# A two-layer encoder on one core: split weight tiles in rows of 136 elements instead of 128

## The chip, the cores and the metric

The kernel runs on one core of one Trainium2 chip, as one launch. TensorE (PE) multiplies, VectorE (DVE) and ScalarE (ACT) prepare operands and take results away, GpSimd (POOL) builds a few tables, and SyncE (SP) issues the loads. The on-chip memory SBUF has 128 partitions; an address in it is given here as bytes from the start of a partition. PSUM takes the products.

The metric is the device time of the launch in microseconds. Before the change the median of two runs is 2129.01 us (2128.55 to 2129.46).

## The reference

An encoder of two layers over 256 tokens and 2048 features, in float32:

```python
def reference(x, attn_norm, mlp_norm, w_mlp_in, w_mlp_out, even_w_in, even_rpb, even_w_out,
              odd_w_qkv, odd_sink, odd_w_out, final_norm):
    for i in range(DEPTH):
        h = rms_norm(x, attn_norm[i])
        j = i // 2
        if i % 2 == 0:
            x = x + even_mixer(h, even_w_in[j], even_rpb[j], even_w_out[j])
        else:
            x = x + odd_mixer(h, odd_w_qkv[j], odd_sink[j], odd_w_out[j])
        x = x + sq_relu_mlp(rms_norm(x, mlp_norm[i]), w_mlp_in[i], w_mlp_out[i])
    return rms_norm(x, final_norm)
```

A mixer is a projection to queries, keys and values, attention with 16 heads of 128 (neighbourhood and dilated windows in layer 0, a window of 128 tokens with grouped keys in layer 1), and a projection back. The MLP is `relu(h @ w1)` squared, times `w2`, with 8192 hidden features. Nearly all the arithmetic is in the weight products.

## The kernel before, in words

Features lie on partitions, tokens along the row. A product's weights are the stationary operand, a tile of 128 x 128 (a k-tile is one such tile of the contraction); the activations of 256 tokens stream past it. To keep float32 accuracy from products of the type float32r, each operand is split into an upper part (rounded to float32r) and a lower one (the rest). Upper and lower parts of an activation lie side by side, so one product with the weights' upper part `h` streams 512 columns (L142), and a second with the weights' lower part `l` streams the upper activations alone, 256 columns (L144). The names of the streamed tiles tell the stage: `u` (normed input of a projection or of the MLP's first product), `hid` (the MLP's hidden features), `o` (heads' outputs). A weight unit, 16 k-tiles and one column block of output, goes through `unit` or `some_units` and `k_range`.

Weights come in halves of a unit: `take_half` issues one load of 512 KB into a tile `r` (SP, six buffers) and splits it into `h` (ACT, L81) and `l` (DVE, L82), five buffers each, up to three halves ahead of their use. A few units at stage changes keep their last two k-tiles in tiles of their own, `hh` and `hl`. At the start three units run in step with the first loads (L463 and L465).

Value projections work the other way round (`value_pair`, L264): the activations are stationary, and two k-tile places of `h` or `l` side by side stream as 256 columns, which needs the half as one flat run of 1024 elements.

Everything is emitted by plain loops, and each engine works through its own queue in that order. Attention's steps are put some steps later into the same order (`later`, `tick`).

Where the tiles lie, as the built program places them: `u` starts at byte 32,896, k-tile k of it 2048k further; `h` tiles at 99,744 plus multiples of 4096, `l` tiles at 120,224 plus multiples of 4096, k-tile k in them 512k further; `hid` and `o` start at 158,208, again 2048 per k-tile. Modulo 512 that is 128 for `u`, 0 for `hid` and `o`, and 416 for every k-tile of weights.

Of the kernel before, what the change touches and what calls it, by code (L numbers as in the profile page):

```python
# [8 lines left out]
F32R = mybir.dt.float32r  # L9
# [5 lines left out]
P = 128  # L15
T = 256
# [8 lines left out]
SCALE = 128.0 ** -0.5  # L25
TW = 384
HALF = KT // 2
RAW_BUFS = 6
PART_BUFS = 5
# steps between the stages of a head's attention  # L30
LAGS_0 = (5,4,3)
LAGS_1 = (4,5,3)
LAGS_END = (3,3,2)
# [7 lines left out]
def encoder(ctx: ExitStack, tc: tile.TileContext, a: dict, outT: bass.AP):  # L41
# [4 lines left out]
    whi = ctx.enter_context(tc.tile_pool(name="whi", bufs=PART_BUFS))  # L46
    wlo = ctx.enter_context(tc.tile_pool(name="wlo", bufs=PART_BUFS))
    held_w = ctx.enter_context(tc.tile_pool(name="held_w", bufs=3))
    work = ctx.enter_context(tc.tile_pool(name="work", bufs=3))
    acc_ps = ctx.enter_context(tc.tile_pool(name="acc_ps", bufs=3, space=PSUM))  # L50
    aux_ps = ctx.enter_context(tc.tile_pool(name="aux_ps", bufs=1, space=PSUM))

# [1 line left out]
    xs = const.tile([P, KT, T], F32, name="xs")  # L54
    u = const.tile([P, KT, 2, T], F32R, name="u")
    g = const.tile([P, 5, KT], F32, name="g")
# [15 lines left out]
    nc.vector.memset(eps, EPS)  # L72

    def warm(func, after):
        # has the function's table loaded ahead of its use
        nc.scalar.activation(warmed, after, func)

    warm(AF.Sqrt, eps)
# [1 line left out]
    def split(hi, lo, src):  # L80
        nc.scalar.activation(hi, src, AF.Copy)  # L81
        nc.vector.tensor_sub(lo, src, hi.bitcast(F32))  # L82

# [1 line left out]
    AHEAD = 2  # L85
    pending = []
    loaded = []

    def need(units, held=0):
        # of the first `held` units the last two k-tiles get tiles of their own  # L90
        for i, src in enumerate(units):
            pending.extend([(src[:, :HALF, :], HALF), (src[:, HALF:, :], HALF - 2 if i < held else HALF)])

    def take_half():
        while pending and len(loaded) <= AHEAD:
            src, n = pending.pop(0)
            r = raw.tile([P, HALF, P], F32, name="r")
            nc.sync.dma_start(r, src)
            h = whi.tile([P, HALF, P], F32R, name="h")
            l = wlo.tile([P, HALF, P], F32R, name="l")  # L100
            split(h[:, :n, :], l[:, :n, :], r[:, :n, :])
            tiles = [(h[:, k, :], l[:, k, :]) for k in range(n)]
            if n < HALF:
                h, l = (held_w.tile([P, 2, P], F32R, name=name) for name in ("hh", "hl"))
                split(h, l, r[:, n:, :])
                tiles += [(h[:, k, :], l[:, k, :]) for k in range(2)]
            loaded.append((h, l, tiles))
        return loaded.pop(0)
# [1 line left out]
    def take_unit():  # L110
        return take_half()[2] + take_half()[2]

# [1 line left out]
    now = [0]  # L114
    tasks = []

# [35 lines left out]
        done(ps)  # L152

    def some_units(done, act):
        # the last k-tiles of the activations become ready late: leave them for the end
        ps = [acc_ps.tile([P, 2 * T], F32, name="acc") for _ in done]
        parts = []
        for i in range(len(done)):
            parts.append(take_unit())
            if act is not u:  # L160
                assert heads_done >= set(range(KT - 2))
            k_range(ps[i], parts[i], act, range(KT - 2))
        if act is not u:
            finish_tasks()
        for i in range(len(done)):
            k_range(ps[i], parts[i], act, range(KT - 2, KT))
            done[i](ps[i])
# [5 lines left out]
        nc.vector.tensor_add(z, ps[:, :T], t)  # L173
        return z

# [1 line left out]
    def gained(k, which):  # L177
        x, gk = xs[:, k, :], g[:, which, k:k + 1]
        if which == 4:
# [14 lines left out]
    norm = {"ready": False, "waiting": []}  # L194

    def finish_norm(last=None, to=None):
        # mean square with tokens on partitions, 1/rms there, and the same along every partition
        ps = aux_ps.tile([P, 512], F32, name="m_ps", bufs=2)
        parts = [ssq] if last is None else [ssq, last]
        for j in range(2):  # L200
            for n, part in enumerate(parts):
                nc.tensor.matmul(ps[:, j:j + 1], part[:, j * P:(j + 1) * P], ones[:, 0:1],
                                 start=n == 0, stop=n == len(parts) - 1)
        r0, v, e = (work.tile([P, 2], F32, name=n, bufs=1) for n in ("r0", "v", "e"))
        nc.scalar.activation(r0, ps[:, :2], AF.Sqrt, bias=eps, scale=1.0 / D)
        nc.vector.tensor_scalar(v, ps[:, :2], 1.0 / D, EPS, op0=ALU.mult, op1=ALU.add)
        nc.vector.reciprocal(r0, r0)
        nc.vector.scalar_tensor_tensor(e, r0, -0.5, r0, op0=ALU.mult, op1=ALU.mult)
        nc.vector.tensor_mul(e, e, v)
        nc.vector.scalar_tensor_tensor(rcol, e, 1.5, r0, op0=ALU.add, op1=ALU.mult)  # L210
        diag = work.tile([P, 2, P], F32, name="diag", bufs=1)
        for j in range(2):
            nc.vector.tensor_scalar(diag[:, j, :], ident, rcol[:, j:j + 1], None, op0=ALU.mult)

        def along():
            out = aux_ps.tile([P, 512], F32, name="m_ps", bufs=2)
            nc.tensor.matmul(out[:, :T], ones, diag.rearrange("p j t -> p (j t)"), start=True, stop=True)
            to(out[:, :T])
        return along
# [13 lines left out]
        later(2, finish_norm(to=to))  # L233
        norm["ready"] = False

# [1 line left out]
    def head_parts(pool, name, bufs, scale, keep):  # L237
        def done(ps):
            z = joined(ps)
# [11 lines left out]
        return done  # L251

    def value_pair(pool, keep):
        # tokens on partitions, two heads at a time
        ps = acc_ps.tile([P, 2, T], F32, name="acc")
        for half in range(2):
            parts = [take_half()[:2] for _ in range(2)]
            for kk in range(HALF):
                k = half * HALF + kk
                h, l = (w.rearrange("p k c -> p (k c)")[:, (kk % 4) * T:(kk % 4 + 1) * T] for w in parts[kk // 4])  # L260
                for j in range(2):
                    js = slice(j * P, (j + 1) * P)
                    for n, (x, y) in enumerate(((0, h), (0, l), (1, h))):
                        nc.tensor.matmul(ps[:, j, :], u[:, k, x, js], y,  # L264
                                         start=k == 0 and j == 0 and n == 0,
                                         stop=k == KT - 1 and n == 2, skip_group_check=True)
                if kk % 2 == 1:
                    tick()
        assert norm["ready"]
        w = pool.tile([P, 2, 2, T], F32R, name="v", bufs=1)  # L270
        for j in range(2):
            nc.scalar.activation(w[:, 0, j, :], ps[:, j, :], AF.Copy, scale=rcol[:, j:j + 1])
            nc.vector.scalar_tensor_tensor(w[:, 1, j, :], ps[:, j, :], rcol[:, j:j + 1],
                                           w[:, 0, j, :].bitcast(F32), op0=ALU.mult, op1=ALU.subtract)
        keep.append(w)

    def attend(pool, o, head, q, k, v, side, biases, lags, sunk=False):
        """q, k, v: lists that hold the operands once their units are done."""
        def scores():
            if not q or not k:  # L280
                later(1, scores)
# [120 lines left out]
                    final = which_next == 4 and b == 1 and c == KT - 1  # L402
                    unit(added(c, final), hid, srcs=2, summed=final)

# [1 line left out]
    w0, w1 = a["even_w_in"], a["odd_w_qkv"]  # L406
    for p in range(8):
        base = 2 * p if p < 4 else 24 + 2 * (p - 4)
        for i in range(2):
            need([w0[base + i], w0[base + 8 + i]])  # L410
        need([a["even_w_v"][p, i] for i in range(2)])
    need([a["even_w_out"][c] for c in range(KT)], 3)

    def mlp_units(layer):
# [5 lines left out]
    mlp_units(0)  # L420
    for p in range(2):
        need([w1[NH + 2 * p + i] for i in range(2)], 2 if p == 0 else 0)
        need([a["odd_w_v"][p, i] for i in range(2)])
        need([w1[8 * p + i] for i in range(8)])
    need([a["odd_w_out"][c] for c in range(KT)], 3)
    mlp_units(1)

# [1 line left out]
    wps = aux_ps.tile([P, 512], F32, name="m_ps", bufs=2)  # L429
    for _ in range(10):  # L430
        nc.tensor.matmul(wps[:, :P], ones, ones, start=True, stop=True)

# [1 line left out]
    STARTERS = 3  # L434
    GROUPS = ((0, 2), (2, 4), (4, 8), (8, 12), (12, 16))
    starters = [[pending.pop(0)[0] for _ in range(2)] for _ in range(STARTERS)]
# [12 lines left out]
    hl = [None] * STARTERS  # L449
    for k0, k1 in GROUPS:  # L450
        ks = slice(k0 % HALF, (k1 - 1) % HALF + 1)
        if k0 % HALF == 0:
            hl = [(whi.tile([P, HALF, P], F32R, name="h"), wlo.tile([P, HALF, P], F32R, name="l"))
                  for _ in range(STARTERS)]
        for i in range(STARTERS):
            split(hl[i][0][:, ks, :], hl[i][1][:, ks, :], rs[k0 // HALF][i][:, ks, :])
# [3 lines left out]
        for i in range(STARTERS):  # L460
            h, l = hl[i]
            for k in range(k0, k1):
                nc.tensor.matmul(sps[i], h[:, k % HALF, :], u[:, k].rearrange("p a t -> p (a t)"),  # L463
                                 start=k == 0, stop=False)
# [9 lines left out]
        later(1 + gi, some_squares(gi))  # L474
    later(8, norm_for_heads)

# [1 line left out]
    with tc.tile_pool(name="attn0", bufs=1) as pool:  # L478
        o = pool.tile([P, NH, 2, T], F32R, name="o")
        sl = slopes(8)  # L480
# [22 lines left out]
        for p in range(8):  # L503
            q, k, v = [[], []], [[], []], []
# [15 lines left out]
        finish_tasks()  # L520
    mlp(0, 2)

# [1 line left out]
    with tc.tile_pool(name="attn1", bufs=1) as pool:  # L524
        o = pool.tile([P, NH, 2, T], F32R, name="o")
        sl = slopes(16)
# [28 lines left out]

    mlp(1, 4)

# [1 line left out]
    def to(r):  # L559
        for k0, k1 in ((0, 1), (1, 2)) + tuple((k, k + 2) for k in range(2, KT, 2)):  # L560
            ks = slice(k0, k1)
# [70 lines left out]
```

## Time and profile before

| | |
|---|---|
| median of the runs | 2129.01 us |
| profiled execution, span from first to last instruction | 2127.8 us |
| PE busy | 2104.8 us (99%), 12438 products |
| DVE busy | 1340.4 us (63%) |
| ACT busy | 1035.6 us (49%) |
| DMA | 386.06 MB, mean 181 GB/s |
| mean granted TensorE clock | 0.994 |

The profiled execution is a run of its own; the profile gives its span, and no other time of it is known. PE is the matrix engine's products, PEld its weight loads, which overlap products. Products are pipelined and the ends that the profile shows for them are modelled, so a product's pace is read from the starts of neighbours. The granted clock is 1.00 at the level of 2.4 GHz and 0.50 at that of 1.2 GHz.

### The profile page before, as it was taken

How to read it: one execution, taken by the hardware profiler on the slowest of the kernel's cores; microseconds unless marked ns; L12 is line 12 of the kernel's file. 1: busy time of each engine (PE TensorE's matmuls, PEld its weight loads, DVE VectorE, ACT ScalarE, POOL GpSimd, SP SyncE). 2: the span in 40 equal slices, each digit the busy share in tenths (PEclk: the TensorE clock that was granted, in tenths of full speed). 3: DMA queues.
4: the chain of work that ended last, by engine and by line, in shares of the span. 5: the costliest groups of instructions: out<-in, count | busy, mean ns of one | idle time of the engine just before them, and what ended most of it. 6: DMA issues, size and time to landing. Idle time of an engine off the chain costs nothing.

```text
span 2127.8 us, 31825 instructions
## 1 busy us (share of the span) xinstructions
PE 2104.8 (99%) x12438; PEld 1852.0 (87%) x12438; DVE 1340.4 (63%) x2088; ACT 1035.6 (49%) x1602; POOL 23.2 (1%) x33
## 2 busy tenths in 40 slices
PE   8999999999999999999999999999999999999997
PEld 6999998888888888888888998888888888888887
DVE  6766676766655556665656877766655556665554
ACT  6555555544444444444445656544444444444442
POOL 2100000000000000000000000000000000000000
PEclk9999999999999999999999999999999999999998
DMA  9754455555555555555555444555555555555552
GB/s 258 180 171 168 168 170 176 190 180 188 187 187 188 188 186 185 187 187 189 188 188 187 148 162 143 188 185 188 185 187 187 188 188 186 187 188 188 188 188 90
DMA packets 108294, 386.06 MB, mean 181 GB/s; under 512 B 12352, under 2 KB 13392, under 8 KB 108144
## 3 DMA queue, kind: packets, MB, share of 16 engines
q1 hardware_dynamic: 106992, 381.73, 53.2%
q0 software_dynamic: 1008, 2.27, 1.5%
q8 instruction: 97, 1.59, 0.3%
q14 instruction: 53, 0.43, 0.1%
q10 hardware_dynamic: 144, 0.04, 0.0%
HBM read 381.89 MB, written 2.10 MB: 180 GB/s over the span
## 4 chain that ended last, share of the span: by engine, by line
PE 96%; DMA 2%; DVE 1%; SPq 0%; ACT 0%; issue 0%; DVEq 0%; ACTq 0%
PE acc L142 58%; PE acc L144 30%; PE acc L264 5%; PE s_ps L288 1%; PE m_ps L332 1%; DMA r<-in_even_w_in 1%; PE p_ps L313 1%; DMA r<-in_even_w_v 1%; DMA xs<-in_xT 0%; ACT h L81 0%; DVE l L82 0%; DVE xs L562 0%; SPq L440 0%; PE acc L140 0%; PE acc L139 0%
## 5 line engine op out<-in xcount | busy, mean ns | idle before, releaser
L82 DVE TENSOR_TENSOR l<-r,h 128x1024 fp32r<-128x1024 f32 (+3 forms) x729 | 880.8, 1209 | 718.4 <-ACT h L81 716.3
L81 ACT ACTIVATE h<-r 128x1024 fp32r<-128x1024 f32 (+3 forms) x729 | 761.5, 1045 | 985.3 <-PE acc L142 646.9
L142 PE MATMUL acc<-u,h 128*128 128x512 f32 x2820 | 1001.0, 397 | 0.0
L144 PE MATMUL acc<-u,l 128*128 128x256 f32 x2820 | 793.8, 281 | 0.0
L142 PE MATMUL acc<-hid,h 128*128 128x512 f32 x2016 | 705.8, 393 | 0.0
L142 PEld LDWEIGHTS acc<-u,h 128*128 128x128 f32 x2820 | 529.7, 188 | 126.9
L144 PE MATMUL acc<-hid,l 128*128 128x256 f32 x2048 | 571.5, 279 | 0.0
L144 PEld LDWEIGHTS acc<-u,l 128*128 128x128 f32 x2820 | 531.7, 189 | 0.2
L142 PEld LDWEIGHTS acc<-hid,h 128*128 128x128 f32 x2016 | 377.7, 187 | 90.3
L144 PEld LDWEIGHTS acc<-hid,l 128*128 128x128 f32 x2048 | 383.7, 187 | 0.0
L142 PE MATMUL acc<-o,h 128*128 128x512 f32 x500 | 176.2, 394 | 1.1 <-DVE z L173 1.1
L144 PE MATMUL acc<-o,l 128*128 128x256 f32 x500 | 139.6, 279 | 0.0
L264 PE MATMUL acc<-h,u 128*128 128x256 f32 x640 | 119.6, 283 | 0.0
L173 DVE TENSOR_TENSOR z<-acc,t 128x256 f32<-128x256 f32 x275 | 114.4, 418 | 2.2 <-ACT t L171 2.1
L142 PEld LDWEIGHTS acc<-o,h 128*128 128x128 f32 x500 | 93.7, 187 | 23.7 <-DVE z L173 1.7
L171 ACT ACTIVATE t<-acc 128x256 f32<-128x256 f32 x275 | 100.5, 366 | 5.5 <-PE acc L144 2.7
L264 PEld LDWEIGHTS acc<-h,u 128*128 128x128 f32 x640 | 100.9, 190 | 0.5
L144 PEld LDWEIGHTS acc<-o,l 128*128 128x128 f32 x500 | 93.7, 187 | 0.0
L264 PE MATMUL acc<-l,u 128*128 128x256 f32 x320 | 90.0, 281 | 0.0
L264 PEld LDWEIGHTS acc<-l,u 128*128 128x128 f32 x320 | 60.9, 190 | 0.1
L374 DVE SCALAR_TENSOR_TENSOR z<-z 128x256 f32<-128x256 f32 x128 | 54.4, 426 | 4.2
L82 DVE TENSOR_TENSOR hid<-z,hid 128x256 fp32r<-128x256 f32 x128 | 53.4, 419 | 1.3 <-ACT hid L81 1.2
(94 smaller groups left out, 859.3 us busy)
## 6 DMA issues: line engine op xcount, KB each, us to landing
r<-in_w_mlp_in SPq DMA_DIRECT2D x256, 512.0 KB, 4.2
r<-in_w_mlp_out SPq DMA_DIRECT2D x256, 512.0 KB, 4.5
r<-in_even_w_in SPq DMA_DIRECT2D x58, 512.0 KB, 3.8
r<-in_odd_w_qkv SPq DMA_DIRECT2D x40, 512.0 KB, 3.7
r<-in_even_w_v SPq DMA_DIRECT2D x32, 512.0 KB, 3.7
r<-in_even_w_out SPq DMA_DIRECT2D x32, 512.0 KB, 3.7
r<-in_odd_w_out SPq DMA_DIRECT2D x32, 512.0 KB, 3.7
r<-in_odd_w_v SPq DMA_DIRECT2D x8, 512.0 KB, 4.2
```

The costliest lines, as they stand in the source:

```text
L81: nc.scalar.activation(hi, src, AF.Copy)
L82: nc.vector.tensor_sub(lo, src, hi.bitcast(F32))
L142: nc.tensor.matmul(ps, h, act[:, k].rearrange("p a t -> p (a t)"), start=start, stop=False)
L144: nc.tensor.matmul(ps[:, :T], l, act[:, k, 0, :], start=False, stop=stop)
L171: nc.scalar.activation(t, ps[:, T:], AF.Copy)
L173: nc.vector.tensor_add(z, ps[:, :T], t)
L264: nc.tensor.matmul(ps[:, j, :], u[:, k, x, js], y, start=k == 0 and j == 0 and n == 0, stop=k == KT - 1 and n == 2, skip_group_check=True)
L288: nc.tensor.matmul(s_ps[:, i, :], qh[:, x, qs], kh[:, y, :], start=n == 0, stop=n == 2)
L313: nc.tensor.transpose(p_ps[:, j, i * P:(i + 1) * P], s[:, i, j * P:(j + 1) * P], ident)
L332: nc.tensor.matmul(o_ps[:, :T], vv[:, x, j, side * P:(side + 1) * P], pt[:, y, j, :], start=n == 0, stop=n == 5)
L374: nc.vector.scalar_tensor_tensor(z, z, 0.0, z, op0=ALU.max, op1=ALU.mult)
```

## The change

A new constant `ROW` is 136. The tiles `h` and `l` get rows of 136 elements per k-tile, of which 128 are used: 544 bytes from one k-tile's weights to the next in place of 512. The split writes 8 rows of 128 into them where it wrote one run of 1024. The halves for the value products are marked `flat` and keep the run of 1024 at the start of the larger tile. The tiles `hh`, `hl` and `r` keep their size. The rest of the diff takes comments and docstrings away.

```diff
 HALF = KT // 2
+ROW = P + 8
...
-    def need(units, held=0):
-        # of the first `held` units the last two k-tiles get tiles of their own
+    def need(units, held=0, flat=False):
+
         for i, src in enumerate(units):
-            pending.extend([(src[:, :HALF, :], HALF), (src[:, HALF:, :], HALF - 2 if i < held else HALF)])
+            pending.extend([(src[:, :HALF, :], HALF, flat),
+                            (src[:, HALF:, :], HALF - 2 if i < held else HALF, flat)])
 
     def take_half():
         while pending and len(loaded) <= AHEAD:
-            src, n = pending.pop(0)
+            src, n, flat = pending.pop(0)
             r = raw.tile([P, HALF, P], F32, name="r")
             nc.sync.dma_start(r, src)
-            h = whi.tile([P, HALF, P], F32R, name="h")
-            l = wlo.tile([P, HALF, P], F32R, name="l")
+            h = whi.tile([P, HALF, ROW], F32R, name="h")
+            l = wlo.tile([P, HALF, ROW], F32R, name="l")
+            if flat:
+                h, l = (w.rearrange("p k c -> p (k c)")[:, :HALF * P] for w in (h, l))
+                split(h, l, r.rearrange("p k c -> p (k c)"))
+                loaded.append((h, l, None))
+                continue
+            h, l = h[:, :, :P], l[:, :, :P]
             split(h[:, :n, :], l[:, :n, :], r[:, :n, :])
...
-                h, l = (w.rearrange("p k c -> p (k c)")[:, (kk % 4) * T:(kk % 4 + 1) * T] for w in parts[kk // 4])
+                h, l = (w[:, (kk % 4) * T:(kk % 4 + 1) * T] for w in parts[kk // 4])
...
-        need([a["even_w_v"][p, i] for i in range(2)])
+        need([a["even_w_v"][p, i] for i in range(2)], flat=True)
...
-        need([a["odd_w_v"][p, i] for i in range(2)])
+        need([a["odd_w_v"][p, i] for i in range(2)], flat=True)
...
-            hl = [(whi.tile([P, HALF, P], F32R, name="h"), wlo.tile([P, HALF, P], F32R, name="l"))
+            hl = [(whi.tile([P, HALF, ROW], F32R, name="h")[:, :, :P], wlo.tile([P, HALF, ROW], F32R, name="l")[:, :, :P])
                   for _ in range(STARTERS)]
```

Each engine's instructions stand in the same order as before, as many and with the same waits; only the shape of the split's operands differs (8 x 128 for 1024). In the built program the `h` tiles then start at 99,744 plus multiples of 4352, the `l` tiles at 121,504 plus multiples of 4352, and `hid` and `o` at 160,768; `u` stays at 32,896.

## Rows read from the trace of the kernel before

**Rows 1.** The page's table of engines: busy us (share of the span) xinstructions.

```profile
PE 2104.8 (99%) x12438; PEld 1852.0 (87%) x12438; DVE 1340.4 (63%) x2088; ACT 1035.6 (49%) x1602; POOL 23.2 (1%) x33
```

**Rows 2.** PE's groups by shape: xcount | busy us, mean ns | idle before.

```profile
L142 PE MATMUL acc<-u,h 128*128 128x512 f32 x2820 | 1001.0, 397 | 0.0
...
L142 PE MATMUL acc<-hid,h 128*128 128x512 f32 x2016 | 705.8, 393 | 0.0
...
L142 PE MATMUL acc<-o,h 128*128 128x512 f32 x500 | 176.2, 394 | 1.1 <-DVE z L173 1.1
...
L142 PE MATMUL acc<-u,hh 128*128 128x512 f32 x12 | 4.4, 397 | 0.0
L142 PE MATMUL acc<-o,hh 128*128 128x512 f32 x12 | 4.3, 393 | 0.0
```

**Rows 3.** L142 alone, by stretch: us, PE busy (count) PEld busy, clock, DMA, GB/s.

```profile
430.00:600.00 170.00, 169.80 (x481) 90.11 (x480) 1.00 0.54 185
610.00:780.00 170.00, 170.00 (x487) 90.92 (x487) 1.00 0.56 187
...
1420.00:1590.00 170.00, 170.00 (x482) 90.37 (x482) 1.00 0.56 187
```

**Rows 4.** Timeline of PE, layer 0's hidden units: start us, duration us, what.

```profile
495.97 0.40 PE L142 MATMUL acc<-u,h 128*128 128x512 f32 x1
496.21 0.28 PE L144 MATMUL acc<-u,l 128*128 128x256 f32 x1
496.33 0.39 PE L142 MATMUL acc<-u,h 128*128 128x512 f32 x1
496.56 0.28 PE L144 MATMUL acc<-u,l 128*128 128x256 f32 x1
496.68 0.40 PE L142 MATMUL acc<-u,h 128*128 128x512 f32 x1
```

**Rows 5.** Timeline of PE, layer 1's projections; four pairs between these are left out.

```profile
1203.07 0.39 PE L142 MATMUL acc<-u,h 128*128 128x512 f32 x1
...
1204.80 0.39 PE L142 MATMUL acc<-u,h 128*128 128x512 f32 x1
```

**Rows 6.** Timeline of PE, layer 0's output units; five pairs are left out.

```profile
700.28 0.39 PE L142 MATMUL acc<-hid,h 128*128 128x512 f32 x1
...
702.38 0.39 PE L142 MATMUL acc<-hid,h 128*128 128x512 f32 x1
```

**Rows 7.** Timeline of PE, the units at the start; three pairs are left out.

```profile
20.90 0.63 PE L463 MATMUL acc<-u,h 128*128 128x512 f32 x1
...
23.46 0.63 PE L463 MATMUL acc<-u,h 128*128 128x512 f32 x1
```

**Rows 8.** All engines in that stretch: PE, PEld, DVE, ACT, POOL busy, then clock.

```profile
18.00:24.00 6.00, 5.37 (x16) 3.94 (x16) 5.92 (x14) 4.68 (x11) 0.30 (x1) 0.50 1.01 217
```

**Rows 9.** DVE's groups by shape: xcount | busy us, mean ns | idle before.

```profile
L82 DVE TENSOR_TENSOR l<-r,h 128x1024 fp32r<-128x1024 f32 x702 | 860.9, 1226 | 703.2 <-ACT h L81 701.4
...
L82 DVE TENSOR_TENSOR hid<-z,hid 128x256 fp32r<-128x256 f32 x128 | 53.4, 419 | 1.3 <-ACT hid L81 1.2
...
L82 DVE TENSOR_TENSOR pt<-p_ps,pt 128x512 fp32r<-128x512 f32 x32 | 21.7, 679 | 0.3 <-ACT pt L81 0.3
...
L562 DVE TENSOR_TENSOR xs<-xs,m_ps 128x512 f32<-128x512 f32 x7 | 4.3, 681 | 0.0
```

**Rows 10.** All engines in two stretches: PE, PEld, DVE, ACT, POOL busy, clock, DMA.

```profile
45.00:325.00 280.00, 276.89 (x1892) 255.26 (x1891) 191.34 (x354) 147.35 (x264) 11.28 (x13) 0.99 0.56 175
...
1146.00:1320.00 174.00, 173.37 (x1138) 157.35 (x1136) 132.38 (x319) 103.22 (x216) 0.00 (x0) 1.00 0.46 156
```

**Rows 11.** DVE's work on tile l alone in the same stretches: busy us (count).

```profile
45.00:325.00 280.00, 108.16 (x89) 0.99 0.56 175
...
1146.00:1320.00 174.00, 62.05 (x52) 1.00 0.46 156
```

## The prediction

> **What bounds the kernel now.** The first view is the page's table of engines: PE is busy 99% of a span of 2127.8 us [rows 1]. The page says that ends of matmuls are modelled, so that number tells only that PE never stands still for long; what PE achieves has to be read from the starts. The second view, the groups of instructions by shape, says what PE does: L142 and L144 in turn, a product of 512 columns with the upper part of a weight tile and one of 256 columns with the lower part. I call the two a pair. There are 2820 pairs that stream u, 2016 that stream hid and 500 that stream o [rows 2], and 24 more on held tiles (12 on u, 12 on o), 5360 in all. Every operation that the change touches feeds or is one of these.
>
> The third view gives the pace of a pair, stage by stage: L142 alone, counted in stretches. In layer 0's hidden units (430 to 600 us) 481 pairs start in 170 us, 353.4 ns each; in its output units (610 to 780) 487 in 170 us, 349.1; in layer 1's hidden units (1420 to 1590) 482 in 170 us, 352.7 [rows 3]. One more or less at an edge is 0.7 ns. So 5360 pairs at about 351 ns are 1881 us of the span: whatever the change does must show in this one number.
>
> The fourth view is the timeline of PE, where the reader should look at starts and ignore durations. Streaming u in layer 0, starts alternate: a pair of 0.36 us (495.97 to 496.33), then one of 0.35 (to 496.68) [rows 4]. Streaming u in layer 1 around 1203 us, the same shapes run evenly: five pairs from 1203.07 to 1204.80, 0.346 each [rows 5]. Streaming hid, six pairs from 700.28 to 702.38, 0.350 each [rows 6]. At the start, while the granted clock is 0.50, the 1.2 GHz level [rows 8], four pairs take from 20.90 to 23.46, 0.640 each [rows 7]. That is the important row: at half the clock 768 columns take 640 ns, so at 2.4 GHz they would take 320 if nothing else came in. They take 346 to 361. Some 31 ns per pair, 166 us of the run, are lost to something that appears at the full clock alone. It is no wait for another engine: PE is busy throughout [rows 1].
>
> **The change part by part.**
>
> *Rows of 136 elements in h and l.* The start of k-tile k's weights moves from 512k to 544k bytes behind the tile's start. Before, all these starts are equal modulo 512 and k only swaps the two halves of 1024; activations lie at multiples of 2048, so all pairs of a stage have one relation modulo 512 between weights and activations (288 for u, 416 for hid and o). Afterwards it steps by 32 per k-tile and covers many values. No row shows that relation varied freely. The nearest is that u and hid, same shapes and same weight tiles, differ by 353 against 349 [rows 3]: another start of the activations goes with 1% of pace. The alternating and the even pace of u at the same addresses [rows 4, 5] say that the moment also matters: a pattern can lock in and stay. Bounds per pair, then: 320 ns at the bottom [rows 7], nothing lost; 361 at the top, the slow half of the alternation in every pair from 495.97 to 496.33 [rows 4]. Between ends so far apart I take the value of the rows nearest to a mixture. A relation that changes with every k-tile gives the alternation of u nothing regular to lock on; I put u's pairs at the pace of hid, 349.1, which is neither its fast nor its slow phase. Hid's and o's pairs already run near the middle of what is seen, and I leave them there. Gain: 2832 x (352.7 - 349.1) = 10.2 us.
>
> *The split writes rows with gaps.* ACT and DVE now write 8 rows of 128 in place of one run of 1024. Per split DVE takes 1226 ns for 1024 elements and 419 for 256, so 1.05 ns an element and 150 ns fixed [rows 9]. Upper bound: each of 7 further rows pays the fixed part, 1.05 us. In 45 to 325 us that adds 89 x 1.05 = 93 to DVE's 191 of 280, and in 1146 to 1320 us 52 x 1.05 = 55 to 132 of 174 [rows 10, 11]: 5 and 13 us over the stretch, some 20 us on the whole. Lower bound: nothing, and the nearest row says so: L562 reads one operand as two repeated rows and takes 681 ns for 512 elements, where the plain split takes 679 [rows 9]. I take nothing. A few tens of ns per split stay hidden behind PE, since DVE is at most 76% busy in these stretches; without that cover 702 splits at 50 ns would be 35 us.
>
> *Addresses behind the tiles.* Ten tiles grow by 256 bytes, so what is allocated behind them shifts by 2560, a multiple of 512. The value products keep the flat layout, with other tile starts alone; 10 pairs of heads x 16 k-tiles x 6 are 960 of them, and 2 ns either way, what separates neighbours in the timeline, would be 2 us. No instruction, load, wait or queue place is added or taken away, and the loads go to tiles r, which stay as they are. Nothing for these.
>
> Sum: the span of 2127.8 less 10 is 2118. The median of the runs, 2129.0, lies 1.2 above the profiled span, so I forecast **2119**.
>
> **A rule against the change.** The pace of u and hid differs by 1% with nothing but the address of the streamed operand different [rows 3], which speaks for some dependence. The Trainium skill says the opposite (SBUF — State Buffer, "Who interferes with whom"): the matmul's streamed operand and the weight load have read ports of their own, and PE waits for nobody. By that rule the change would leave the time at 2129; the half-clock row agrees with it [rows 7], the two paces at the full clock do not [rows 3]. The Trainium skill (TensorE: Matmul & The Clock Gate, "Back-to-back issue gap") gives N/2.4 + 2.5 ns at the full clock, 325 ns for a pair; an estimate from it, 5360 x 26, puts the most that could be won at 139 us.
>
> **The rivals.**
>
> *Nothing happens.* If the loss of 31 ns is not a matter of addresses at all, but of the moment at which loads and streams meet, a new row length shifts moments and not the mean. For it: two paces at the same addresses [rows 4, 5]. Against it: u and hid [rows 3]. Time 2129, give or take 5.
>
> *The loss goes away.* If weight load and stream meet in the same part of the memory because their starts are a power of two apart, spreading the starts removes a good part of it. For it: the loss exists, 166 us, and hits every pair alike. Against it: the two starts already differ by 288 in one stage and by 416 in the other, and the loss is there in both; and the stream passes over 1024 or 2048 bytes during a load of 512, so it meets the load's region wherever it starts. Half of the loss gone gives 2129 - 83 = 2046. It decides by over 2% from a mean pair of 343 ns down (351 less 42.6 us / 5360).
>
> *The slow phase becomes the rule.* Today each pair's relation is one of two values; among 16 or more there will be bad ones. If these hold PE in the slow phase, every pair takes what every second one takes in the alternation of u: 2832 x (361 - 352.7) + 2528 x (361 - 349.1) = 54 us, 2183, slower than before. From a mean pair of 359 up it is over 2%. For it: the slow phase is real and stays for long stretches [rows 4]. Against it: hid never shows it [rows 6].
>
> *Gaps in the rows slow the split.* The upper bound above: about 2150, within 2% of before.
>
> **How the numbers follow.** Chances: forecast 0.44, with 2100 (every pair at the even 346 [rows 5] would give 2102) to 2129 as its own range; nothing happens 0.22; loss goes away 0.18; slow phase 0.13, a little of it short of 2%; slower split 0.03. Over 2% either way, which is about what a measurement of this kernel can tell from no change, is below 2086 or above 2172. Faster 0.18, slower 0.12, the same 0.70. The range must leave out no more than 0.2: from 2070, which cuts off the larger part of the case in which the loss goes away (0.1), to 2172, which cuts off the slow phase's end (0.1 at most).
>
> **What would show it.** The number of L142 in 170 us: 487 in both stages for the forecast, 481 and 487 for nothing, over 500 if the loss goes, 471 if the slow phase rules. DVE's mean for 128x1024 should stay at 1226 ns. In the timeline the regular alternation of [rows 4] should be gone. The forecast is wrong if u's count doesn't rise, if hid's moves by more than 5, or if PE shows waits for DVE l that it doesn't have now.

## The result, and the profile after

The changed kernel takes 2113.01 us (median of 2112.73 and 2113.29), before 2129.01: a ratio of 0.9926 with a 95% interval of 0.9897 to 0.9955, 16 us faster. That is clear of noise and within 2%.

The page's table of engines, first line, answers to [rows 1]:

```profile
PE 2088.1 (99%) x12438; PEld 1846.7 (87%) x12438; DVE 1339.8 (63%) x2088; ACT 1036.6 (49%) x1602; POOL 23.0 (1%) x33
```

PE is as busy as before, with the same number of products, over a span of 2111.4 us instead of 2127.8. DVE's and ACT's busy times haven't moved. The 16 us are in the pace of PE.

The pace by stretch, as in [rows 3] (L142 is L150 now, L144 is L152): us, PE busy (count), PEld busy (count), clock, DMA share, GB/s.

```profile
430.00:600.00 170.00, 169.80 (x488) 91.39 (x487) 1.00 0.57 187
610.00:780.00 170.00, 170.00 (x489) 91.68 (x488) 1.00 0.58 189
1420.00:1590.00 170.00, 170.00 (x489) 91.67 (x488) 1.00 0.58 189
```

u went from 481 and 482 pairs to 488 and 489, hid from 487 to 489: the stages now run alike. For single nanoseconds I also took the mean difference between neighbouring starts over the whole trace (pairs followed by another pair, without those over 380 ns). Before: 353.0 ns for u, 350.0 for hid, 350.1 for o; after: 348.5, 348.3 and 348.4. With 2832, 2016 and 512 pairs that is 12.7 + 3.4 + 0.8 = 16.9 us, the whole difference of the spans (16.4); the value products take 0.5 us more than before.

The timeline of PE in layer 0's output units (start us, duration us, what; the products of 256 between are left out) stands where [rows 6] stood:

```profile
701.83 0.40 PE L150 MATMUL acc<-hid,h 128*128 128x512 f32 x1
...
702.18 0.39 PE L150 MATMUL acc<-hid,h 128*128 128x512 f32 x1
...
702.53 0.39 PE L150 MATMUL acc<-hid,h 128*128 128x512 f32 x1
...
702.88 0.39 PE L150 MATMUL acc<-hid,h 128*128 128x512 f32 x1
...
703.22 0.39 PE L150 MATMUL acc<-hid,h 128*128 128x512 f32 x1
...
703.56 0.40 PE L150 MATMUL acc<-hid,h 128*128 128x512 f32 x1
...
703.92 0.40 PE L150 MATMUL acc<-hid,h 128*128 128x512 f32 x1
...
704.27 0.39 PE L150 MATMUL acc<-hid,h 128*128 128x512 f32 x1
...
704.62 0.40 PE L150 MATMUL acc<-hid,h 128*128 128x512 f32 x1
```

The reader should take differences of starts: 0.35, 0.35, 0.35, 0.34, 0.34, 0.36, 0.35, 0.35. It is a pattern of eight pairs, one for each distance between weights and activations modulo 256 (192, 224, 0, 32, 64, 96, 128, 160), and it lasts 2.79 us, 0.349 a pair.

DVE's groups by shape, as in [rows 9], and a line of what PE waited for (engine, line, waited for: us in total, times, longest us):

```profile
L83 DVE TENSOR_TENSOR l<-r,h 128x1024 fp32r<-128x1024 f32 x702 | 860.6, 1226 | 688.7 <-ACT h L82 686.2
...
L570 DVE TENSOR_TENSOR xs<-xs,m_ps 128x512 f32<-128x512 f32 x7 | 4.3, 680 | 0.0
```

```profile
PE acc L473 <- DVE l L83: 0.2, 1, 0.2
```

The split into rows with gaps costs DVE what the flat one did, 1226 ns. PE waits for it once, at the start, for 0.2 us; before, the view had no such line. All of PE's waits for other engines in that view add up to 14.4 us before and 14.7 after.

### The profile page after: what moved, and what is told of

It is laid out like the page before. It is cut to its first block, busy times and chain, and to the rows that moved or that the text cites. A ratio compares the mean times of both kernels' runs of the same rounds, so it can differ in the third digit from the quotient of the medians.

```text
span 2111.4 us, 31825 instructions
## 1 busy us (share of the span) xinstructions
PE 2088.1 (99%) x12438; PEld 1846.7 (87%) x12438; DVE 1339.8 (63%) x2088; ACT 1036.6 (49%) x1602; POOL 23.0 (1%) x33
## 4 chain that ended last, share of the span: by engine, by line
PE 96%; DMA 2%; DVE 1%; ACT 0%; SPq 0%; issue 0%; DVEq 0%; ACTq 0%
PE acc L150 58%; PE acc L152 30%; PE acc L272 5%; PE s_ps L296 1%; PE m_ps L340 1%; DMA r<-in_even_w_in 1%; PE p_ps L321 1%; DMA r<-in_even_w_v 1%; DMA xs<-in_xT 0%; ACT h L82 0%; DVE l L83 0%; DVE xs L570 0%; PE acc L147 0%; PE acc L148 0%; PE m_ps L225 0%
## 5 line engine op out<-in xcount | busy, mean ns | idle before, releaser
L150 PE MATMUL acc<-u,h 128*128 128x512 f32 x2820 | 988.4, 394 | 0.0
L152 PE MATMUL acc<-u,l 128*128 128x256 f32 x2820 | 788.6, 280 | 0.0
L150 PE MATMUL acc<-hid,h 128*128 128x512 f32 x2016 | 702.4, 393 | 0.0
L150 PEld LDWEIGHTS acc<-u,h 128*128 128x128 f32 x2820 | 529.9, 188 | 119.2
L152 PE MATMUL acc<-hid,l 128*128 128x256 f32 x2048 | 572.3, 279 | 0.0
L152 PEld LDWEIGHTS acc<-u,l 128*128 128x128 f32 x2820 | 529.1, 188 | 0.2
L150 PEld LDWEIGHTS acc<-hid,h 128*128 128x128 f32 x2016 | 378.7, 188 | 87.3
L152 PEld LDWEIGHTS acc<-hid,l 128*128 128x128 f32 x2048 | 384.1, 188 | 0.0
L150 PE MATMUL acc<-o,h 128*128 128x512 f32 x500 | 175.2, 394 | 1.1 <-DVE z L181 1.1
L152 PE MATMUL acc<-o,l 128*128 128x256 f32 x500 | 139.8, 280 | 0.0
L150 PEld LDWEIGHTS acc<-o,h 128*128 128x128 f32 x500 | 93.9, 188 | 22.8 <-DVE z L181 1.7
L152 PEld LDWEIGHTS acc<-o,l 128*128 128x128 f32 x500 | 93.8, 188 | 0.0
```

The costliest lines, as they stand in the source:

```text
L150: nc.tensor.matmul(ps, h, act[:, k].rearrange("p a t -> p (a t)"), start=start, stop=False)
L152: nc.tensor.matmul(ps[:, :T], l, act[:, k, 0, :], start=False, stop=stop)
```

## The experiments

"Distance" is the start of a weight tile less the start of the operand streamed past it, modulo 256 bytes. The question was whether u gained because its distance had been a bad one, or because a distance that keeps changing is good in itself; and whether the order of distances matters. Where a text below says starts of L144, the starts of the 512-column products were counted, one to a pair as well. The MLP of a layer takes its hidden features in two halves, so hidden units (u) and output units (hid) come twice in each layer. The fences show L142's counterpart in 170 us stretches of the hidden and the output units of layer 0's first half, columns as above, and paces without a fence are means over neighbouring starts as above; where a stream's pace is not the same in all stages, the text says so. The kernel before was run beside each group and had medians of 2127.2, 2129.5, 2128.7 and 2127.1 us.

**Fixed distances.** Rows of 128, and small pads that shift tiles:

```diff
...
+    pad_w = ctx.enter_context(tc.tile_pool(name="pad_w", bufs=1)).tile([P, 8], F32, name="pad_w")
+    nc.vector.memset(pad_w, 0.0)
     raw = ctx.enter_context(tc.tile_pool(name="raw", bufs=RAW_BUFS))
...
+    pad_a = ctx.enter_context(tc.tile_pool(name="pad_a", bufs=1)).tile([P, 24], F32, name="pad_a")
+    nc.vector.memset(pad_a, 0.0)
     work = ctx.enter_context(tc.tile_pool(name="work", bufs=3))
...
```

*64 everywhere.* 

> Rows of 128 as before; two small pads shift the weight tiles by 32 bytes and hid and o by 128, so that every weight tile starts at 64 modulo 256 behind the streamed operand, in all stages and for all k-tiles. Theory A (the distance between the starts of weights and streamed operand, modulo 256 bytes, sets the pace; changing it helps only because it visits better distances): from the changed kernel's trace, 226.3 ns for a 512 whose weights lie at 64 and 113.7 for the 256 ahead of weights at 64, 340 a pair, 2129 - 2832 x 13 - 2528 x 10 = 2067 us. Theory B (any fixed distance locks into a bad pattern, variation itself helps): 349 to 353 a pair, 2120 to 2130 us.

Measured 2137.6 us, ratio 1.0051 (1.0036 to 1.0066).

```profile
430.00:600.00 170.00, 169.72 (x480) 90.24 (x480) 1.00 0.56 185
610.00:780.00 170.00, 170.00 (x482) 90.47 (x482) 1.00 0.57 187
```

Theory A, which I had drawn from the best class in the changed kernel's trace, is wrong: pairs at 64 take 341.7 ns there (hid) and 353.3 here. The same distance has another price when its neighbours have the same distance. Theory B said 2120 to 2130 us and missed too, by 8 us: its pace was at the top of its band, 353.2 for u and 353.3 for hid.

*128 everywhere* (pads of 24 and 8 elements). 

> As the kernel with 64, but every weight tile at 128 modulo 256. Theory A: 236.4 and 119.1 ns, 355.5 a pair, 2150 us. Theory B: 349 to 353 a pair, 2120 to 2130 us, the same as with 64.

Measured 2127.4 us, ratio 1.0004 (0.9994 to 1.0014).

```profile
430.00:600.00 170.00, 169.80 (x484) 90.72 (x484) 1.00 0.57 185
610.00:780.00 170.00, 170.00 (x485) 90.97 (x485) 1.00 0.57 188
```

351.0 ns for u, 351.1 for hid. Again not A's number; B's band holds here, but B said the two fixed kernels would be alike, and they differ by 10 us.

*Distances of u and hid exchanged* (pads of 32 and 32). 

> Rows of 128 as before; the pads give u's weights the distance that hid's had (160 modulo 256) and hid's and o's that of u (32). Theory A: the pace goes with the distance: u even at 349 to 350 a pair (486 or 487 starts of L144 in 170 us of hidden units), hid at 353 (481 or 482), partly alternating 361 and 346; about 2128 us. Theory C (the alternation belongs to the stage that streams u, not to addresses): 481 and 487 as before.

Measured 2127.1 us, ratio 0.9999 (0.9989 to 1.0010). The third line is layer 1's hidden units, the last its output units (160 us).

```profile
430.00:600.00 170.00, 169.48 (x485) 90.59 (x484) 1.00 0.57 186
610.00:780.00 170.00, 170.00 (x492) 92.03 (x491) 1.00 0.58 189
1420.00:1590.00 170.00, 170.00 (x486) 90.93 (x486) 1.00 0.58 189
...
1590.00:1750.00 160.00, 160.00 (x454) 84.99 (x454) 1.00 0.57 186
```

u at 160 runs as hid did, 350.1 ns. hid at 32 runs at 346.7 through all of layer 0, where theory A had 353, and at 353.3, alternating, through all of layer 1; o at 32 alternates in both layers. So the alternation of [rows 4] goes with the distance of 32 and not with u; and that distance has two patterns, of which the MLP's stages take up one at their start and keep it. This settles that addresses count, against theory C and against the rival that nothing happens. The Trainium skill (SBUF — State Buffer, "Who interferes with whom") gives streams and weight loads separate ports and lets PE wait for nobody; here the pace of the same products of u went with where the two operands lie, 353.0 ns at 32 and 350.1 at 160, and the measurement decides. Which part of PE loses the time no run shows.

*h at 64, l at 128* (pads of 8, 16 and 8). 

> Rows of 128; tiles h at 64 and tiles l at 128 modulo 256 behind every streamed operand. Theory A1 (what counts is the load under way while a product streams, that is the next weights): products of 512, under which l is loaded, take 236, products of 256, under which the next h is loaded, 114; 350 a pair, 2121 us. Rival A2 (what counts is the product's own weights): 512 takes 226 and 256 takes 118; 344 a pair, 2088 us.

One run, 2124.0 us. The timeline of PE, 512-column products alone:

```profile
640.17 0.40 PE L148 MATMUL acc<-hid,h 128*128 128x512 f32 x1
...
640.53 0.39 PE L148 MATMUL acc<-hid,h 128*128 128x512 f32 x1
...
640.87 0.40 PE L148 MATMUL acc<-hid,h 128*128 128x512 f32 x1
...
641.23 0.39 PE L148 MATMUL acc<-hid,h 128*128 128x512 f32 x1
```

It alternates, 0.36 and 0.34; the pairs are 233 + 123 and 228 + 116 ns. Their mean, 350.0, is A1's sum, but neither A1's parts (236 + 114) nor A2's (226 + 118) are there. Which of the two loads meets which stream stays open.

*0 for u and 96 for hid; 192 and 224* (pads of 56 and 16; 40 and 48). 

> Rows of 128, two pads: u's weights at a fixed distance of 0 modulo 256, hid's and o's at 96. The four fixed distances measured so far gave 353.0 (32), 353.3 (64), 351.1 (128) and 350.0 ns (160). Theory G (any fixed distance settles at 350 to 353): both in that band, 2126 to 2136 us. Theory F (among the other four there is a fast one, which a fixed distance could use for all): one of the two at 347 or less, seen by 490 or more starts of L144 in 170 us of its stage.

> As before with 192 for u and 224 for hid and o. Theory G: both at 350 to 353, 2126 to 2136 us. Theory F: one at 347 or less.

Measured 2116.7 us, ratio 0.9942 (0.9922 to 0.9963), and 2114.4, ratio 0.9932 (0.9912 to 0.9952). Of the first, then of the second; the third line of each is the hidden units of the MLP's second half (160 us):

```profile
430.00:600.00 170.00, 169.47 (x488) 91.40 (x489) 1.00 0.57 188
610.00:780.00 170.00, 170.00 (x491) 92.02 (x491) 1.00 0.58 189
790.00:950.00 160.00, 160.00 (x454) 85.06 (x454) 1.00 0.56 186
```

```profile
430.00:600.00 170.00, 169.80 (x487) 91.42 (x486) 1.00 0.57 188
610.00:780.00 170.00, 170.00 (x491) 91.94 (x490) 1.00 0.58 190
790.00:950.00 160.00, 160.00 (x454) 85.12 (x453) 1.00 0.58 186
```

Theory F holds: hid at 96 and at 224 runs at a steady 346.7 ns. u at 0 takes 350.4 in the mean over the run and at 192 351.4, but each is a mixture. In the hidden units of the MLP's first half u settles at 346.7 (distance 0) and 348.9 (192), in those of the second half at 353.3 in both kernels, and both layers repeat this. So 0 and 192 have two paces each, as 32 has, though the tiles lie at the same places in both halves. The changed kernel shows no such difference; its hidden units of the second half in layer 0, against 488 in the first:

```profile
790.00:960.00 170.00, 170.00 (x490) 91.69 (x489) 1.00 0.58 189
```

**One part of the change alone.** Rows of 136 in h, 128 in l:

```diff
...
-            l = wlo.tile([P, HALF, ROW], F32R, name="l")
+            l = wlo.tile([P, HALF, P], F32R, name="l")
...
```

> One part of the change alone: rows of 136 in the tiles h, rows of 128 in the tiles l, so that only the upper parts' distances step by 32 and l stays at 32 (u) or 160 (hid, o) modulo 256. Theory B (a distance that changes from pair to pair keeps the slow patterns from settling): half of the loads vary, about half of the gain or all of it, 2113 to 2121 us. Theory E (only the loads of l, which run under the products of 512, matter): no gain, 2125 to 2130 us.

Measured 2120.7 us, ratio 0.9959 (0.9945 to 0.9974).

```profile
430.00:600.00 170.00, 169.80 (x486) 90.99 (x485) 1.00 0.57 186
610.00:780.00 170.00, 170.00 (x487) 91.11 (x486) 1.00 0.58 188
```

u at 350.0, hid at 350.0: u leaves its bad pattern with the steps of h alone, hid gains nothing. Theory E is out.

**The same distances in another order.** The changed kernel, the 8 k-tiles of a half taken in steps of 3, 5 or 7 (5 is shown):

```diff
-        for k in ks:
+        ks = list(ks)
+        if len(ks) == KT:
+            ks = [half + 5 * i % HALF for half in (0, HALF) for i in range(HALF)]
+        for n, k in enumerate(ks):
...
```

> The changed kernel, with the 8 k-tiles of each half taken in the order 0, 3, 6, 1, 4, 7, 2, 5: the same tiles at the same places, each distance met as often as before, but a step of 96 from pair to pair instead of 32. Theory B (variation alone): the same as the changed kernel, 2113 us, 348.4 a pair. Theory D (the pace depends on the distance together with the step from the pair before): another pace, anywhere between 342 and 355 a pair, 2080 to 2150 us, more than 5 us from 2113.

Measured 2112.9 us, ratio 0.9928 (0.9911 to 0.9944).

```profile
430.00:600.00 170.00, 169.80 (x488) 91.41 (x487) 1.00 0.58 188
610.00:780.00 170.00, 170.00 (x489) 91.59 (x489) 1.00 0.58 189
```

> As before, order 0, 5, 2, 7, 4, 1, 6, 3: a step of 160, or 96 backwards. Theory B: 2113 us. Theory D: more than 5 us from 2113, and not the time of the step of 96.

Measured 2104.9 us, ratio 0.9887 (0.9872 to 0.9901).

```profile
430.00:600.00 170.00, 169.80 (x490) 91.85 (x490) 1.00 0.58 189
610.00:780.00 170.00, 170.00 (x492) 92.11 (x491) 1.00 0.59 190
```

> As before, order 0, 7, 6, 5, 4, 3, 2, 1: a step of 32 backwards. Theory B: 2113 us. Theory D: more than 5 us from 2113.

Measured 2120.8 us, ratio 0.9962 (0.9947 to 0.9977).

```profile
430.00:600.00 170.00, 169.80 (x486) 90.94 (x485) 1.00 0.57 186
610.00:780.00 170.00, 170.00 (x487) 91.16 (x486) 1.00 0.58 188
```

The three ran on one chip, and the intervals don't overlap. The step of 96 gives what theory B wanted, and there theory D's expectation missed; the steps of 160 and backwards moved the time by 8 us either way with each distance met as often as before. So distances alone don't set the pace: their order counts too, which is theory D, though not every new order gives a new pace. For hid, a pair at 32 takes 343.3 ns in the changed kernel, 344.4 with the step of 96, 340.1 with 160 and 347.0 backwards; one at 160 takes 344.3, 344.4, 346.7 and 356.6. Means: 348.3, 348.4, 346.7 and 350.0.

**Half the step.** `ROW = P + 4`. 

> The changed kernel with rows of 132 elements: a step of 16 bytes from pair to pair. Theory D (the step matters, and every step so far but one that is zero gave 346.7 to 350.0): 346.5 to 350 ns a pair, 2104 to 2122 us. If what counts is whole stretches of 32 bytes, half of the steps change nothing, and the pace comes nearer to that of a fixed distance, 350 to 352 and 2121 to 2130 us.

Measured 2122.3 us, ratio 0.9969 (0.9958 to 0.9980).

```profile
430.00:600.00 170.00, 169.80 (x485) 90.83 (x485) 1.00 0.57 186
610.00:780.00 170.00, 170.00 (x487) 91.11 (x486) 1.00 0.58 188
```

350.3 for u and 350.0 for hid lie at the edge of both expectations; this run tells nothing about a grain of 32 bytes, but it shows that a varying distance need not beat hid's old pace. The step is also not all that differs: a tile is now 4224 bytes long, so successive h tiles start 128 apart modulo 256 in turn, and so do the h and the l of one pair.

**A fixed distance of 96 everywhere** (pads of 16 and 16). 

> Rows of 128, no gaps, two pads of 64 bytes: a fixed distance of 96 modulo 256 in all stages. If the pace goes with the distance and not with the stage, u takes the 346.7 ns that hid took at 96: 2129 - 2832 x 6.2 - 2528 x 3.3 = 2103 us, faster than the changed kernel's 2113, with no varying distance at all. If only the stages of hid and o can run at 346.7, u stays at 350 or more and the time at 2112 or more.

Measured 2106.3 us, ratio 0.9901 (0.9885 to 0.9918).

```profile
430.00:600.00 170.00, 169.80 (x491) 91.80 (x490) 1.00 0.58 188
610.00:780.00 170.00, 170.00 (x492) 92.00 (x491) 1.00 0.58 190
1420.00:1590.00 170.00, 170.00 (x491) 92.11 (x491) 1.00 0.58 189
```

u takes hid's 346.7 ns (346.8), and in every stage of the MLP. The distances 96 and 160 were each met by u and by hid with the tiles at other places, and gave one pace each; as far as these two show, the distance counts and not the place of one operand. The pairs give the 26 us that were expected; 3 come back in the value products, whose weights are the streamed side: from the start of each of its products to the start of the next, L264's counterpart takes 121.4 us in all instead of 118.0. This kernel has rows without gaps and no varying distance, and runs at least as fast as the changed one: its interval and the changed kernel's overlap (0.9885 to 0.9918, 0.9897 to 0.9955), the spans are 2104.9 and 2111.4 us.

## Why the prediction was right, point by point

**What bounds the kernel.** Right. The whole gain is pace of the 5360 pairs; PE's waits (14.4 and 14.7 us) and the other engines' busy times stayed.

**u's pairs go to hid's pace, 10.2 us.** Right in sign and place, a little small: 12.7 us, from 353.0 to 348.5 ns instead of 352.7 to 349.1. The alternation is gone. The reason given was that a pattern can lock in, and that a changing distance leaves it nothing to lock on. The runs bear out the first part: at the fixed distances 0, 32 and 192 a stage settles at one of two paces. The four kernels that step through all eight distances in both loads show one pace each, the same in every stage of the MLP (346.7, 348.3, 348.4, 350.0). But they don't run without a pattern, they repeat one of eight pairs, and it need not be fast. Nor is the change needed for the gain: u also gains at fixed distances (350.1 at 160, 346.8 at 96). By the stages of the MLP the fixed distances take 346.7 or 353.3 (0), 346.7 or 353.3 (32; u before always 353.3), 353.3 (64), 346.7 (96), 351.1 (128), 350.0 (160), 348.9 or 353.3 (192) and 346.7 (224). What the runs show is that u stood at a distance whose usual pattern is among the slowest. A varying distance gives something between the best and the middle of these, and that is a gain for whatever stood at a bad one. That it came out near hid's pace was an assumption without a row, and partly luck: other orders of the same distances moved it 1.6 ns down and 1.7 up.

**hid and o stay.** The term that was mis-sized: put at 0, it measured 1.7 ns a pair, 3.4 + 0.8 us. There was no row from which to know on which side of hid's 350 the mixture would lie; the orders gave 346.7, 348.3, 348.4 and 350.0, from a gain of 3.3 ns to none.

**The split costs nothing.** Right: 1226 ns before and after, so the upper bound of 150 ns a row was far off. The row of L562 pointed the right way, though it reads in two pieces and writes none with gaps. By the letter one sign of a wrong forecast came up, a wait of PE for DVE's l that wasn't there before; it is 0.2 us long and comes once.

**Other addresses.** Right within its 2 us: L264's counterpart takes 118.5 us in all by starts, before 118.0. In other layouts these products moved by more than 2 us, to 121.4 with 96 everywhere and to 115.8 with 192 and 224.

**Rivals.** *Nothing happens* fell with the exchange of distances. *The loss goes away* fell: no distance and no order brought a stage's mean under 346.7 ns, against 320 at no loss [rows 7]; single pairs reach 340.1. Its argument against, that a stream passes the load's place from wherever it starts, fits with that but was not tested by itself. *The slow phase becomes the rule* fell too; the slowest steady pace of any stage of the MLP was 353.3. Its counterargument, that hid never alternates, holds for hid's distance and not for hid: moved to 32, hid alternated through layer 1. *A slower split* is out by DVE's time.

**Open.** Why a distance of 96 is good and one of 64 bad, what the remaining 27 ns of a pair are, and what decides which pattern a stage takes up at its start. The even stretch of u before [rows 5] begins right behind a break by attention's transposes (L313, at 1201.93 us), while the pairs just before that break alternate (0.34, 0.36 and 0.35 us); the moment of a break may have a part in it, which no run tested.

## What to carry to other kernels

Where PE is busy 99% and the starts of equal products are farther apart in one stage than in another, compare where weights and streamed operands lie in SBUF: pads of 32 to 224 bytes ahead of tiles moved this kernel between 1.0% faster and 0.5% slower. Price a distance in a steady run of its own, not from a kernel in which it alternates with others; what a class costs in a mixture did not carry over. And price it in every stage: three of eight fixed distances had two paces in one execution. If distances can't be chosen, steps that visit all of them took away the worst case here (350.0 at most, against 353.3), and a good fixed one did as well with less code.

## What the runs showed of the hardware that was not expected

In the changed kernel's trace hid's pairs fall into eight classes by distance modulo 256 bytes; within a class the pairs, some 252 each, differ by a standard deviation of 0.0 to 0.9 ns, whatever tile, k-tile or half they come from, while the class means go from 341.7 to 355.0. A period of 512 or 1024 explains nothing more.

A fixed distance can have two steady paces: hid at 32 took 346.7 ns in layer 0 and 353.3 in layer 1 of one execution, u at 0 took 346.7 in the first half and 353.3 in the second half of each layer's MLP, and u at 192 348.9 and 353.3.

The patterns that repeat last 346.7 or 353.3 ns (one pair), 693.3, 700.0 or 706.7 (two), 1046.7, 1053.3 or 1060.0 (three), 2773.3, 2786.7 or 2800.0 (eight); these are all multiples of 6.67 ns. I have no run that says of what.
